# A delta-rule recurrence's triangular system: three products on the right-hand side in place of the block inverse

## The chip, the cores and the metric

One Trainium2 chip, one core. The metric is the device time of one launch in microseconds. The kernel before took 2555.1 us (median of three runs, 2553.93 to 2557.61). Times in the text are microseconds; positions such as "1572 us" count from the start of the profiled execution's span.

## The reference, cut to what matters

The program is two blocks on a sequence of 256 tokens and 2048 channels in float32. The first block has two gated-linear-attention and pooling layers; the second has a mixer of an RWKV-7 group (16 heads of 64) beside a sparse-attention group, then cross attention and an MLP. The change touches the RWKV-7 recurrence alone:

```python
def step(state, inp):
    r_t, w_t, k_t, v_t, kk_t, a_t = inp
    sa = jnp.einsum('bhvk,bhk->bhv', state, -kk_t)
    state = (state * w_t[:, :, None, :]
             + sa[..., None] * (kk_t * a_t)[:, :, None, :]
             + v_t[..., None] * k_t[:, :, None, :])
    return state, jnp.einsum('bhvk,bhk->bhv', state, r_t)
```

The state is read by every step before it is updated, so a chunk of tokens computed at once leads to a triangular system: with N the strictly lower-triangular matrix of the scores between the removal keys within the chunk (128x128 for each head), one needs G = (I - N)^-1 applied to a right-hand side.

## The kernel before, in words

The whole program is one launch. Python code emits instructions, and a planner at build time fixes the order of each engine's queue from the program order, estimated costs and free buffers; semaphores between the engines are generated. Big projections (`project`) stream weights from HBM in 512 KB pieces, split them on ScalarE (L148) and VectorE (L154) into two parts and multiply three times (L163 to L165). The planner fills these products into holes of other stages.

`rwkv_half(hf, ...)` (L1269) handles 8 of the 16 heads, and is called twice: for the first half at L1546, for the second at L1665. Its steps are: decay and key preparation on all engines; the score products `psa` for all heads and both chunks of 128 tokens (L1402, kept in `sas`); the inverse of every 32x32 diagonal block of I - N, for all heads at once, by 30 steps on VectorE (L1407 to L1418), with the result in `invt` and, transposed, in `invx`; then, for two head groups of four heads each (`heads4`, L1422), the rest of the solve and the output. The two groups run as coroutines that take turns at each `yield` (`together`, L1510), so their instructions alternate in program order. Each goes through the chunks t = 0 and t = 1 in order, as the state s0 of the first enters the second. At t = 0 the right-hand side has 64 columns per head (the values), at t = 1 it has 128 (the values and the keys that meet the state).

For one head group and one chunk, the solve before the change is this. `spread` (L1431) puts the 32x32 block inverses on the diagonal of a 128x128 matrix per head: `wt` from `invt`, `xt` from `invx`. Then two levels, l = 5 (blocks of 64) and l = 6 (blocks of 128): `pz` = N times xt (L1451), masked to the level's off-diagonal blocks into `zt` (L1453), `pw` = zt times wt (L1457), added to `wt` (L1458). Between the levels `wt` is transposed on TensorE (`px`, L1445) and copied by ScalarE to `xt` (L1447). Then `pk` (L1462) makes the right-hand side `rhs` (L1464, and L1467 on GpSimd for t = 1), and `pg` = wt times rhs (L1471) is copied to `ga` (L1473). What follows, the masked scores `psr`/`sr`, `py`, `pst` and `s0`, isn't touched. All these tiles of 128x512 have tag "m", of which there are nine buffers; all PSUM results have tag "side", of which there are three. An fp32 product is two passes of TensorE, and each shows as an instruction.

After both groups are through, VectorE normalises y and the rope work of the attention projections follows; the latter shares a tag of two buffers ("rp") with the states s0.

Of the kernel before, what the change touches and what calls it, by code (L numbers as in the profile page):

```python
# [12 lines left out]
AL = mybir.AluOpType  # L13
# [11 lines left out]
C_IDENT, C_LT, C_GT, C_ONES, C_BD32, C_LE, C_SEL2, C_SEL4, C_FREQ, C_SEL8, C_ID32, C_ALL = (  # L25
    0, 128, 256, 384, 512, 640, 768, 770, 772, 796, 828, 860)
# [28 lines left out]
def tile_kernel(ctx: ExitStack, tc: tile.TileContext, I: dict, out: bass.AP):  # L55
    nc = tc.nc
    V, S, G, PE = nc.vector, nc.scalar, nc.gpsimd, nc.tensor
# [25 lines left out]
    def tl(tag, shape=None, dt=F, name=None):  # L83
        pool, (n, bufs) = (sb, BASE[tag]) if tag in BASE else (phase[1], phase[2][tag])
        shape = [128, n] if shape is None else shape
        return pool.tile(shape, dt, name=name or tag, tag=tag, bufs=bufs)

    def pconst(shape, name, dt=F):
        return phase[1].tile(shape, dt, name=name, bufs=1)

    def psum(tag, shape=None, name=None):
        return phase[3].tile(shape or [128, 512], F, name=name or tag, tag=tag, bufs=phase[4][tag])
# [4 lines left out]
    def pside(shape=None, name="side"):  # L97
        return psum("side", shape, name)
# [4 lines left out]
    def const(shape, name, dt=F):  # L103
        return sb.tile(shape, dt, name=name, bufs=1)
# [3 lines left out]
    cst = const([128, C_ALL], "cst")  # L108
    nc.sync.dma_start(cst[:, :128], I["cst"][:, :128])
    ident = cst[:, C_IDENT:C_IDENT + 128]  # L110
# [361 lines left out]
    for g in range(4):  # L472
        m = tl("g", [128, 2, 512], name="mem")
# [50 lines left out]
    for j, (t0, nt) in enumerate(PARTS):  # L524
# [15 lines left out]
        for cb in range(4):  # L540
            acc = [pacc() for _ in range(4)]
            for k0 in range(t0, t0 + nt, 2):
                wh, wl = load_w(we, k0, 2, cb * 512, 512)
                for t in range(4):
                    x = uT if t < 2 else ucT
# [20 lines left out]
    lev = const([128, 7 * 128], "lev", U8)  # L566
# [39 lines left out]
    for d in range(2):  # L606
        for half in range(2):
            w = gate_w(d, half)
            la = []
            for t in range(2):  # L610
                px = pside()
                PE.matmul(px, rT[:, 1, t * 128:(t + 1) * 128], w, start=True, stop=True)
                x = tl("h", name="lac")
# [281 lines left out]
    for p in range(2):  # L895
# [12 lines left out]
        for q in (0, 2):  # L908
            pt = transpose2(lambda t, kt: of[:, t, kt * 128:(kt + 1) * 128], q)
            h, l = ybT.h[p][:, q:q + 2], ybT.l[p][:, q:q + 2]  # L910
# [93 lines left out]
    class Rows:  # L1004


        n = 4
# [194 lines left out]
    seg2 = tl("c", name="seg2")  # L1202
    G.memset(seg2, 1.0)
    G.memset(seg2.rearrange("p (n c) -> p n c", c=128)[:, :, 0:1], 0.0)
    strict = cst[:, C_LT:C_LT + 128]
    upto = cst[:, C_LE:C_LE + 128]
    bc4 = lambda m: m[:, None, :].to_broadcast([128, 4, 128])
# [61 lines left out]
    def rwkv_half(hf, kx, rx, vx):  # L1269
# [6 lines left out]
        for dst, p0, b0 in ((sgm, 0, W0), (av, 64, A0)):  # L1276
            for q in (0, 2):
                pd = pside([128, 2, T], name="pd")
                for r in range(2):
                    PE.matmul(pd[:, r], wup[p0:p0 + 64, (q + r) * 128:(q + r + 1) * 128], lora[p0:p0 + 64, 0],  # L1280
                              start=True, stop=True)
# [101 lines left out]
        def scores(dst, qx_, mask, hg, t, name):  # L1383

            ps = [pside([128, 2, 2, 128], name="p" + name) for _ in range(2)]
            for n, kx_ in enumerate((av, kx)):
                for c in range(2):
                    for o in range(2):
                        PE.matmul(ps[o][:, n, c], head(kx_, hg, 2 * c + o, t), head(qx_, hg, 2 * c + o, t), start=True, stop=True)
            for o in range(2):  # L1390
                V.tensor_tensor(dst(o).rearrange("p a b i -> p (a b) i"), ps[o].rearrange("p a b i -> p (a b) i"), bc4(mask),
                                op=AL.mult)
# [15 lines left out]
        for j in range(1, 31):  # L1408
            n = 31 - j
# [5 lines left out]
        invt = tl("g", [128, 32, 32], name="invt")  # L1415
        invx = tl("g", [128, 32, 32], name="invx")
# [5 lines left out]
        def heads4(hg):  # L1422
            s0 = None
            for t in range(2):
                tok = slice(t * 128, (t + 1) * 128)
                hv = slice(hg * 256, hg * 256 + 256)
                sa = sas[t, hg]
                nt_ = lambda i: sa[:, i % 2, 0, i // 2]
                b0 = (t * 2 + hg) * 4

                def spread(x, name):  # L1431
                    d = tl("m", [128, 4, 128], name=name)
                    V.tensor_tensor(wide(d), x[:, :, b0:b0 + 4].rearrange("p i h -> p h i")[:, :, None, :].to_broadcast([128, 4, 4, 32]),
                                    wide(bc4(cst[:, C_BD32:C_BD32 + 128])), op=AL.mult)
                    return d


                wt = spread(invt, "wt")
                xt = spread(invx, "xt")
                for l in range(5, 7):  # L1440
                    yield
                    if l == 6:
                        px = pside([128, 4, 128], name="px")
                        for i in range(4):
                            PE.transpose(px[:, i], wt[:, i], ident)  # L1445
                        xt = tl("m", [128, 4, 128], name="xt")
                        S.copy(xt, px)  # L1447
                        yield
                    pz = pside([128, 4, 128], name="pz")
                    for i in range(4):  # L1450
                        PE.matmul(pz[:, i], nt_(i), xt[:, i], start=True, stop=True)  # L1451
                    zt = tl("m", [128, 4, 128], name="zt")
                    V.tensor_tensor(zt, pz, bc4(lev[:, l * 128:(l + 1) * 128]), op=AL.mult)  # L1453
                    yield
                    pw = pside([128, 4, 128], name="pw")
                    for i in range(4):
                        PE.matmul(pw[:, i], zt[:, i], wt[:, i], start=True, stop=True)  # L1457
                    V.tensor_tensor(wt, pw, wt, op=AL.add)  # L1458
                yield
                pk = pside([128, 4, 64], name="pk")  # L1460
                for i in range(4):
                    PE.matmul(pk[:, i], sa[:, i % 2, 1, i // 2], vn[:, t, hg * 256 + i * 64:hg * 256 + i * 64 + 64], start=True, stop=True)  # L1462
                rhs = tl("m", [128, 4, 128], name="rhs")
                V.tensor_copy(rhs[:, :, :64], pk)  # L1464
                n = 128 if t else 64
                if t:
                    G.tensor_copy(rhs[:, :, 64:], an[:, hv].rearrange("p (h k) -> p h k", h=4))  # L1467
                yield
                pg = pside([128, 4, 128], name="pg")
                for i in range(4):  # L1470
                    PE.matmul(pg[:, i, :n], wt[:, i], rhs[:, i, :n], start=True, stop=True)  # L1471
                ga = tl("m", [128, 4, 128], name="ga")
                S.copy(ga[:, :, :n], pg[:, :, :n])  # L1473
                yield
                sr = [tl("m", [128, 2, 2, 128], name="sr") for _ in range(2)]
                scores(lambda o: sr[o], rx, upto, hg, t, "sr")
                if t:
                    yield
                    pr_ = pside([128, 2, 128], name="pr_")
                    for i in range(4):  # L1480
                        c, o = divmod(i, 2)
                        PE.matmul(pr_[o * 64:o * 64 + 64, c], ga[:, i, 64:], sr[i % 2][:, 0, i // 2], start=True, stop=True)
                    rh = tl("m", [128, 2, 128], name="rh")
                    V.tensor_tensor(rh, pr_, rx[:, hg * 2:hg * 2 + 2, tok], op=AL.add)
                yield
                py = pside([128, 4, 64], name="py")
                for i in range(4):
                    c, o = divmod(i, 2)
                    PE.matmul(py[:, i], sr[o][:, 0, c], ga[:, i, :64], start=True, stop=False)
                    PE.matmul(py[:, i], sr[o][:, 1, c], vn[:, t, hg * 256 + i * 64:hg * 256 + i * 64 + 64], start=False,  # L1490
                              stop=t == 0)
                    if t:
                        PE.matmul(py[:, i], rh[:, c], s0[:, c, o], start=False, stop=True)
                S.copy(y[:, t, hv], flat(py))
                if t == 0:
                    yield
                    pst = pside([128, 2, 64], name="pst")
                    for i in range(4):
                        c, o = divmod(i, 2)
                        hk = slice(hg * 256 + i * 64, hg * 256 + i * 64 + 64)  # L1500
                        PE.matmul(pst[o * 64:o * 64 + 64, c], bn[:, hk], ga[:, i, :64], start=True, stop=False)
                        PE.matmul(pst[o * 64:o * 64 + 64, c], kn[:, hk], vn[:, 0, hk], start=False, stop=True)
                    s0 = tl("rp", [128, 2, 2, 64], name="s0")
                    G.memset(s0, 0.0)
                    for c in range(2):
                        for o in range(2):
                            r = slice(o * 64, o * 64 + 64)
                            S.activation(s0[r, c, o], pst[r, c], AF.Identity, scale=fs[r, hg * 2 + c:hg * 2 + c + 1])

        for _ in together(*[heads4(hg) for hg in range(2)]):  # L1510
            pass
# [221 lines left out]
    for hf in range(2):  # L1733
        for q in (0, 2):
            pt = transpose2(lambda t, kt: yr[hf][:, t, kt * 128:(kt + 1) * 128], q)
            h, l = yrT.h[hf][:, q:q + 2], yrT.l[hf][:, q:q + 2]
# [176 lines left out]
```

## Time and profile before

| | us |
|---|---|
| median of three runs | 2555.1 |
| profiled execution | 2557.92 |
| its span | 2556.2 |
| TensorE matmuls busy | 2422.8 (95%) |
| TensorE weight loads busy | 1928.6 (75%) |
| VectorE busy | 1796.2 (70%) |
| ScalarE busy | 1170.2 (46%) |
| GpSimd busy | 172.1 (7%) |

The page's chain of work that ended last is TensorE for 61% of the span, VectorE for 18% and waits for transfers for 11%. Matmul ends are modelled, so busy TensorE time overlaps itself; the start-to-start times in the chain are the better measure. The two calls of `heads4` run at 1361 to 1412 us and at 1572 to 1619 us.

### The profile page before, as it was taken

What the parts mean: (1) busy time and instruction counts of PE and PEld (TensorE: products, weight loads), DVE (VectorE), ACT (ScalarE), POOL (GpSimd) and SP (SyncE); (2) the same over time, 40 slices, a digit from 0 to 9 for tenths busy, and PEclk for the clock granted to TensorE, in tenths of its full rate; (3) what the DMA queues carried; (4) which work ended last, traced back from release to release, by engine and by line L of the source; (5) the groups of instructions that cost most, each with busy time, mean ns of one, the idle gap of its engine ahead of it and who ended that gap; (6) DMA issues with size and microseconds to landing.
All of it is one profiled execution on the core that took longest, in us unless ns stands there. A gap on an engine that the chain in (4) does not pass through costs nothing.

```text
span 2556.2 us, 32427 instructions
## 1 busy us (share of the span) xinstructions
PE 2422.8 (95%) x11491; PEld 1928.6 (75%) x11491; DVE 1796.2 (70%) x2991; ACT 1170.2 (46%) x1560; POOL 172.1 (7%) x169
## 2 busy tenths in 40 slices
PE   8999998889989998998999999999999999999998
PEld 5667766778767776787878677787888888888886
DVE  5898657997897888967687978755655544555544
ACT  6543244444653544445642452445544433444433
POOL 0000010220230010002020120100000000000000
PEclk9999999999999999999999999999999999999999
DMA  7877547676656788755633243145466555666554
GB/s 262 276 251 225 170 153 242 218 232 228 198 183 218 233 282 288 259 182 158 198 94 110 80 136 99 63 163 192 133 189 182 186 187 187 189 184 187 201 188 154
DMA packets 267358, 483.11 MB, mean 189 GB/s; under 512 B 21137, under 2 KB 45547, under 8 KB 267195
## 3 DMA queue, kind: packets, MB, share of 16 engines
q1 hardware_dynamic: 266875, 480.60, 58.4%
q8 instruction: 90, 1.47, 0.2%
q14 instruction: 73, 0.60, 0.1%
q10 hardware_dynamic: 320, 0.44, 0.1%
HBM read 477.82 MB, written 3.15 MB: 188 GB/s over the span
## 4 chain that ended last, share of the span: by engine, by line
PE 61%; DVE 18%; DMA 11%; issue 6%; ACT 3%; POOL 1%; SPq 0%; DVEq 0%; ACTq 0%; POOLq 0%
PE acc L165 17%; PE acc L164 17%; PE acc L163 17%; DMA ar<-in_w_ada 8%; DVE wl L154 6%; DVE aa L405 3%; PE trp L236 2%; ACT wh L148 1%; DMA lnb<-in_ln_b 1%; PE pw L1457 1%; PE pz L1451 1%; DVE u L1411 1%; DVE inv L1412 1%; DMA wr<-in_w_in_e 1%; DMA wr<-in_w_in_o 0%
## 5 line engine op out<-in xcount | busy, mean ns | idle before, releaser
L148 ACT CAST wh<-wr 128x1024 fp32r<-128x1024 f32 (+2 forms) x736 | 760.3, 1038 | 991.6 <-PE acc L165 804.6
L164 PE MATMUL acc<-wl,xh 128*128 128x512 f32 (+2 forms) x2560 | 1005.5, 393 | 22.9 <-DVE wl L154 22.7
L163 PE MATMUL acc<-wh,xh 128*128 128x512 f32 (+2 forms) x2560 | 1011.8, 396 | 14.1 <-ACT xh L253 6.1
L165 PE MATMUL acc<-wh,xl 128*128 128x512 f32 (+2 forms) x2560 | 1003.5, 393 | 2.4 <-DVE xl L254 1.9
L154 DVE TENSOR_TENSOR wl<-wr,wh 128x512 fp32r<-128x512 f32 (+2 forms) x928 | 622.3, 702 | 176.8 <-ACT wh L148 176.1
L164 PEld LDWEIGHTS acc<-wl,xh 128*128 128x128 f32 x2560 | 485.1, 189 | 135.8 <-DVE wl L154 37.2
L151 DVE TENSOR_TENSOR wl<-wr,wh 128x1024 fp32r<-128x1024 f32 x272 | 333.3, 1225 | 357.4 <-ACT wh L148 355.4
L163 PEld LDWEIGHTS acc<-wh,xh 128*128 128x128 f32 x2560 | 484.6, 189 | 127.1 <-ACT wh L148 10.0
L165 PEld LDWEIGHTS acc<-wh,xl 128*128 128x128 f32 x2560 | 484.8, 189 | 106.3 <-issue 4.0
L405 DVE SCALAR_TENSOR_TENSOR aa<-ar,cs,aa 128x512 f32<-128x512 f32 x240 | 191.0, 796 | 72.8 <-DMA ar<-in_w_ada 71.5
L165 PE MATMUL acc<-wh,ucl 128*128 128x512 f32 x128 | 50.9, 398 | 0.0
L164 PE MATMUL acc<-wl,uch 128*128 128x512 f32 x128 | 50.7, 396 | 0.0
L163 PE MATMUL acc<-wh,uch 128*128 128x512 f32 x128 | 49.8, 389 | 0.0
L381 DVE SCALAR_TENSOR_TENSOR am<-ar,cs,am 128x512 f32<-128x512 f32 x60 | 42.6, 746 | 7.3 <-DMA ar<-in_w_ada 7.3
L722 PE MATMUL pp<-eq,ek 128*128 128x128 f32 x224 | 29.4, 286 | 6.1 <-DVE ek L734 6.1
L722 PEld LDWEIGHTS pp<-eq,ek 128*128 128x128 f32 x224 | 28.5, 201 | 8.4 <-issue 5.0
L1055 POOL TENSOR_TENSOR sgo<-sgo,psc 128x512 f32<-128x512 f32 x8 | 14.6, 1850 | 295.5 <-ACT sgo L1049 164.8
L350 PE MATMUL ada<-wl,c 128*4 128x512 f32 x64 | 26.0, 406 | 4.2 <-DVE wl L154 4.2
L164 PE MATMUL acc<-wl,dh 128*128 128x512 f32 x64 | 26.2, 410 | 3.8 <-DVE wl L154 3.7
L457 DVE SCALAR_TENSOR_TENSOR xl<-trp,pr,xh 128x256 fp32r<-128x256 f32 x48 | 22.3, 480 | 10.1 <-ACT xh L456 9.9
L1866 ACT ACTIVATE un<-acc,rml 128x512 f32<-128x512 f32 x32 | 22.0, 689 | 15.6 <-PE acc L165 15.6
L163 PEld LDWEIGHTS acc<-wh,uch 128*128 128x128 f32 x128 | 24.4, 191 | 5.6
(592 smaller groups left out, 2457.3 us busy)
## 6 DMA issues: line engine op xcount, KB each, us to landing
ar<-in_w_ada SPq DMA_DIRECT2D x288, 256.0 KB
wr<-in_w_in_e SPq DMA_DIRECT2D x128, 512.0 KB
wr<-in_w_up SPq DMA_DIRECT2D x128, 512.0 KB
wr<-in_w_down SPq DMA_DIRECT2D x128, 512.0 KB
wr<-in_w_in SPq DMA_DIRECT2D x80, 512.0 KB
wr<-in_w_in_o SPq DMA_DIRECT2D x64, 512.0 KB
wr<-in_w_ada SPq DMA_DIRECT2D x64, 256.0 KB
wr<-in_w_out_e SPq DMA_DIRECT2D x32, 512.0 KB
```

What stands on the lines that cost most here:

```text
L148: S.copy(wh, wr)
L151: engines[0].tensor_tensor(wl, wr, wh.bitcast(F), op=AL.subtract)
L154: engines[q % 2].tensor_tensor(wl[:, q], wr[:, q], wh[:, q].bitcast(F), op=AL.subtract)
L163: PE.matmul(acc, xh, wh, start=start, stop=False)
L164: PE.matmul(acc, xh, wl, start=False, stop=False)
L165: PE.matmul(acc, xl, wh, start=False, stop=stop)
L236: PE.transpose(pt[:, q, t * 128:(t + 1) * 128], src(t, kt + q), ident)
L350: PE.matmul(acc, c4[:, k0 + q], wl[:, q], start=False, stop=k0 + q == 15)
L381: V.scalar_tensor_tensor(acc[a], w[:, q], col, acc[a], op0=AL.mult, op1=AL.add)
L405: V.scalar_tensor_tensor(acc, w, cs[:, k:k + 1], acc, op0=AL.mult, op1=AL.add)
L722: PE.matmul(pp[:, h, t], kx[:, 2 * h + c, s * 128:(s + 1) * 128], qx[:, 2 * h + c, t * 128:(t + 1) * 128], start=c == 0, stop=c == 1)
L1411: V.tensor_tensor(u, inv[:, j + 1:, j:j + 1].to_broadcast([128, n, j]), inv[:, j:j + 1, :j].to_broadcast([128, n, j]), op=AL.mult)
```

## The change

Off the diagonal blocks no inverse is formed any more. Let D be the block-diagonal matrix of the 32x32 inverses and M = D times the part of N outside the diagonal blocks. Then (I - N)^-1 b equals D applied to a solution that is built from b by repeated multiplication; as four block rows make the fourth power of the block-strict part vanish, three products are enough. `dt` and `dx` are the spread blocks (as wt and xt before). `pmm` multiplies dx with N, and a mask `off32` (one minus the mask of the 32x32 diagonal blocks, a new constant, made once at the start of the phase) keeps the blocks off the diagonal: `mt`. `pk` and `rhs` follow as before. Then x = rhs, and three times x = rhs + M x: `px` on TensorE, the add on VectorE, with a `yield` before each. Last `pg` = dt times x. The transposes, the ScalarE copy, the level masks and the second pair pz/pw are gone.

```diff
+    off32 = pconst([128, 128], "off32")
+    V.tensor_scalar(off32, cst[:, C_BD32:C_BD32 + 128], -1.0, 1.0, op0=AL.mult, op1=AL.add)
...
-                wt = spread(invt, "wt")
-                xt = spread(invx, "xt")
-                for l in range(5, 7):
-                    yield
-                    if l == 6:
-                        px = pside([128, 4, 128], name="px")
-                        for i in range(4):
-                            PE.transpose(px[:, i], wt[:, i], ident)
-                        xt = tl("m", [128, 4, 128], name="xt")
-                        S.copy(xt, px)
-                        yield
-                    pz = pside([128, 4, 128], name="pz")
-                    for i in range(4):
-                        PE.matmul(pz[:, i], nt_(i), xt[:, i], start=True, stop=True)
-                    zt = tl("m", [128, 4, 128], name="zt")
-                    V.tensor_tensor(zt, pz, bc4(lev[:, l * 128:(l + 1) * 128]), op=AL.mult)
-                    yield
-                    pw = pside([128, 4, 128], name="pw")
-                    for i in range(4):
-                        PE.matmul(pw[:, i], zt[:, i], wt[:, i], start=True, stop=True)
-                    V.tensor_tensor(wt, pw, wt, op=AL.add)
+                dt = spread(invt, "dt")
+                dx = spread(invx, "dx")
+                pm = pside([128, 4, 128], name="pmm")
+                for i in range(4):
+                    PE.matmul(pm[:, i], dx[:, i], nt_(i), start=True, stop=True)
+                mt = tl("m", [128, 4, 128], name="mt")
+                V.tensor_tensor(mt, pm, bc4(off32), op=AL.mult)
                 yield
                 pk = pside([128, 4, 64], name="pk")
...
+                x = rhs
+                for _ in range(3):
+                    yield
+                    px = pside([128, 4, 128], name="px")
+                    for i in range(4):
+                        PE.matmul(px[:, i, :n], mt[:, i], x[:, i, :n], start=True, stop=True)
+                    x = tl("m", [128, 4, 128], name="x")
+                    V.tensor_tensor(x[:, :, :n], px[:, :, :n], rhs[:, :, :n], op=AL.add)
                 yield
                 pg = pside([128, 4, 128], name="pg")
                 for i in range(4):
-                    PE.matmul(pg[:, i, :n], wt[:, i], rhs[:, i, :n], start=True, stop=True)
+                    PE.matmul(pg[:, i, :n], dt[:, i], x[:, i, :n], start=True, stop=True)
```

## Rows read from the trace of the kernel before

**Rows 1.** Busy time by stretch: PE, PEld, DVE, ACT, POOL, granted clock, DMA share, GB/s.
```profile
1411.00:1440.00 29.00, 26.11 (x127) 17.54 (x126) 27.86 (x100) 11.77 (x23) 7.06 (x6) 0.94 0.24 66
1440.00:1500.00 60.00, 57.37 (x263) 44.74 (x263) 45.97 (x119) 33.72 (x49) 1.91 (x4) 1.00 0.48 146
1572.00:1592.00 20.00, 17.59 (x137) 16.79 (x138) 11.64 (x18) 1.92 (x4) 0.00 (x0) 0.84 0.00 1
...
1601.00:1619.00 18.00, 17.30 (x159) 15.93 (x157) 8.82 (x17) 3.23 (x6) 1.04 (x1) 1.00 0.06 19
1619.00:1635.00 16.00, 11.20 (x51) 6.60 (x50) 15.73 (x58) 4.86 (x7) 6.18 (x5) 1.00 0.00 2
1660.00:1720.00 60.00, 60.00 (x293) 49.92 (x293) 35.54 (x67) 31.30 (x53) 0.00 (x0) 1.00 0.47 160
```

**Rows 2.** Chain of waits, second half, t = 0: start us, us, what.
```profile
1573.99 3.91 PE pz L1451 x16
1577.90 2.13 PE pw L1457 x16
1580.06 0.70 DVE wt L1458
1580.81 0.66 PE px L1445 x4
1581.46 1.89 PE pz L1451 x16
1583.35 1.94 PE pw L1457 x16
1585.30 1.73 PE pk L1462 x16
1587.03 1.79 PE pg L1471 x16
```

**Rows 3.** Chain of waits, second half, t = 1.
```profile
1599.01 2.20 PE pw L1457 x16
...
1606.46 1.73 PE pk L1462 x16
1608.20 1.84 PE pg L1471 x16
```

**Rows 4.** Chain of waits, first half: level-5 pw, a projection product, pk; then t = 1.
```profile
1367.66 1.78 PE pw L1457 x16
...
1369.68 0.23 PE acc L164
...
1375.80 1.73 PE pk L1462 x16
...
1390.21 1.16 PE pw L1457 x8
...
1398.24 1.73 PE pk L1462 x16
```

**Rows 5.** Timeline, second half, t = 0, one hand-over: start us, us, instruction, idle before.
```profile
1581.30 2.05 PE L1451 MATMUL pz<-xt,sa 128*128 128x128 f32 x16
...
1582.44 0.69 DVE L1453 TENSOR_TENSOR zt<-pz,lev 128x512 f32<-128x512 f32 x1 [1.69 <-PE pz L1451]
1583.19 2.11 PE L1457 MATMUL pw<-wt,zt 128*128 128x128 f32 x16
```

**Rows 6.** Projection products on TensorE in two stretches of the first half: us, busy, count.
```profile
1367.66:1375.80 8.14, 1.88 (x6) 1.00 0.62 184
1390.21:1398.24 8.03, 1.66 (x5) 1.00 0.01 2
```

**Rows 7.** Groups by line and shape, 1572 to 1619: busy us, mean ns, idle before.
```profile
L1451 PE MATMUL pz<-xt,sa 128*128 128x128 f32 x64 | 10.2, 322 | 4.9 <-DVE xt L1433 4.9
L1453 DVE TENSOR_TENSOR zt<-pz,lev 128x512 f32<-128x512 f32 x8 | 5.5, 691 | 5.8 <-PE pz L1451 5.8
...
L1484 DVE TENSOR_TENSOR rh<-pr__13355,rr 128x256 f32<-128x256 f32 x1 | 0.4, 415 | 0.0
```

## The prediction

> **What bounds the kernel now.** I read the page's table of slices first: TensorE is at nine tenths or more almost throughout, so the end belongs to whatever keeps TensorE from its next product, and the question is whether the triangular solve is such a place. So next the busy time by stretch [rows 1]. In the second half the solve runs from 1572 to 1619 us; TensorE is busy 17.59 of 20.00 us and 17.30 of 18.00 us there, VectorE about half the time, ScalarE and the DMA engines hardly at all. Then the chain of waits, read inside the solve in order of time [rows 2 to 4]: it is a sequence of TensorE groups pz, pw, px, pz, pw, pk, pg, each "x16" (two head groups of four heads, two passes for each fp32 product) and each starting where the one before ends. The two head groups alternate: while TensorE works for one, VectorE masks or adds for the other. A hand-over taken from the timeline shows that this just fits [rows 5]: a pair of groups takes 1.89 us, so one group 0.95; pz of group A starts at 1581.30, its mask runs from 1582.44 for 0.69, and pw of A starts at 1583.19, when pz of B has been issued. The solve is therefore bound by the number of TensorE passes, with one hole at the transposes (below). Behind it stand 16 us in which VectorE is the bound (15.73 of 16.00) and which begin when the solve is over, then TensorE without a gap (60.00 of 60.00) [rows 1]; after the first half, VectorE 27.86 of 29.00 and TensorE 57.37 of 60.00. The DMA engines are busy for less than half of these stretches [rows 1], so no transfer should take over as the bound, and what the solve gives up should reach the end.
>
> **What is removed.** For each half of the heads and each token chunk t (four solves): pw of level 5, the add into wt, the transposes px with the ScalarE copy xt, pz of level 6 with its mask, pw of level 6 with its add. In the second half, t = 0, this is the stretch from 1577.90 (pw) to 1585.30 (pk) [rows 2]: 7.40 us, namely 2.13 + 0.70 + 0.66 + 1.89 + 1.94 and the hand-overs. The 0.70 and 0.66 are the hole: eight transposes are too little work to cover the other group's add and copy. For t = 1 it is 1599.01 to 1606.46, 7.45 us [rows 3]. In the first half the same stretch is 1367.66 to 1375.80, 8.14 us, and 1390.21 to 1398.24, 8.03 us [rows 4], but TensorE put six and five products of the projection into it [rows 6], and these must be done in any case. They start 0.23 us apart where the chain shows them alone [rows 4], so 1.4 and 1.15 us come off: 6.75 and 6.9 us.
>
> **What is added.** The old first pz becomes pmm and its mask zt becomes mt: the same eight products, the same 128x512 mask (0.691) [rows 7]; I count no difference. New are three rounds of eight products M x with an add of rhs. For t = 0 the moving side has 64 columns; the nearest rows are pk and pg of the same shape, 1.73 and 1.79 us [rows 2], so 1.76 each, 5.3 for three. For t = 1 it has 128; pg of that shape takes 1.84 [rows 3] and pw 1.94 [rows 2]; I take 1.9, 5.7 for three. pg itself and pk are unchanged. Each round adds a wait: the products of one group wait for VectorE's add of that group, and behind them on TensorE's queue stand the other group's products, then the score products. With 64 columns the add is like rh (128x256 from PSUM, 0.415) [rows 7] and is covered by 0.87 us of the other group; with 128 columns it is the 0.69 us of zt, covered as at that hand-over [rows 5], without a margin to speak of.
>
> **Sum.** Second half: 5.3 - 7.4 = -2.1 and 5.7 - 7.45 = -1.75. First half: 5.3 - 6.75 = -1.45 and 5.7 - 6.9 = -1.2. Together -6.5 us on a path that TensorE sets.
>
> **What counts nothing.** ScalarE loses eight copies of some 0.6 us, but it sits idle in the solve [rows 1]; their effect is in the hole already. VectorE's work per solve goes from eight operations of 0.69 to two of 0.69 and six of 0.42 at t = 0, and stays at eight of 0.69 at t = 1; it has room in the second half, and in the first the weight splits use it. The one new constant off32 is a 128x128 operation, done once, with no neighbour waiting; bound 0 to 0.4 (twice its size, rh, takes 0.415 [rows 7]). The nine buffers of tag m: dt, mt, rhs and x of both groups are eight live tiles, and x of one round takes the place of the last but one, which TensorE has read by then, so I see no wait for a buffer, though with one spare only. pk needs nothing of the inverse any more and stands third instead of sixth among the solve's PSUM tiles. At t = 0 its first half could run in TensorE's idle 4.9 us ahead of the first product [rows 7]: bound 0 to -0.87 us per half, -1.7 in all. I take 0, as its rhs copy would then enter a stretch full of VectorE work.
>
> **Bounds of the disputed price,** a round. Below: pk's 1.73 for both widths, which makes twelve rounds 20.8 us instead of 22.0 (sum -7.7). Above: the add isn't covered at all, and each round shows 0.9 us of VectorE (0.69 and some 0.2 of hand-over, from its times [rows 5]): +10.8 us, sum +4.3. I take the rows' alternation, because pz and pw with the same mask or add run without a hole in it.
>
> [...] A 64-column pass of pk takes 1.73 / 16 = 0.108 us and a 128-column pass of pw 1.94 / 16 = 0.121 [rows 2]: twice the columns, 12% more time. [...]
>
> **Rivals.**
> 1. The rounds wait for the adds: the groups fall out of step (a buffer of tag m released late, or the planner's order putting both adds behind one another), and each of the twelve rounds shows 0.9 us. For it: the hand-over fits [rows 5] within 0.1 us, and one spare buffer; against it: the same handshake holds today. It would give +4.3 us, 2559; it turns the change slower once the waits exceed 0.55 us a round, which is 6.5 / 12.
> 2. The gain is eaten on the way: the planner orders the neighbouring projection and rope work anew, or the first half's part (-2.65) is lost where the projection's products filled holes. -1 to -4.5, about 2552. For it: the first half's TensorE had other work to fill with [rows 6]. Against it: both halves are followed by VectorE at its limit [rows 1].
> 3. pk moves ahead at t = 0 in both halves: -6.5 - 1.7 = -8.2, 2547.
> 4. Time goes with the columns moved: 64-column rounds at half of pw's 1.94, 0.97 instead of 1.76, for six rounds: a further -4.7, -11.2 in all, 2544. pk and pg with 64 columns speak against it.
>
> **How the numbers follow.** The profiled execution took 2557.9 us (span 2556.2), 2.8 above the median of the three runs, 2555.1; the forecast is a difference, so 2555.1 - 6.5 = 2548.6, say 2549. What can't be told from no change is 0.2%, 5.1 us: faster means below 2550.0, slower above 2560.2. Chances: the forecast 0.52 (its own range 2546 to 2551.5), rival 1 0.16, rival 2 0.24, rival 3 0.05, rival 4 0.03. Faster: 0.44 of the forecast's 0.52 and rivals 3 and 4, 0.52. Slower: half of rival 1, in which a round shows more than one add, 0.08, and 0.04 of rival 2, a new order that costs more than all the solves give; 0.12. Same: the rest, 0.36. The range for 8 in 10 goes from rival 4 to just below rival 1: 2543 to 2558.
>
> **What would show it.** In the solve the chain should read pmm, pk, three rounds px, pg, the rounds 1.7 to 1.95 us each for both groups and with no VectorE entry between them. From pg's end to the first product of its solve it should be shorter by 2 us in the second half and by 1.3 in the first, and VectorE's full stretches should follow as much earlier. VectorE's adds between the px entries of the chain, or px's waits above 0.5 us, would show rival 1; solves shorter by 6 us with the same end, rival 2. The forecast is wrong if a round takes over 2.2 us or if the end moves less than the solves.

## The result, and the profile after

The changed kernel took 2570.93 us (median of eight executions, 2568.13 to 2583.57), the kernel before 2556.36 beside it; the ratio is 1.0054, with a 95% interval of 1.0038 to 1.0070. That is 14 us slower by the interval's middle, where 6.5 us faster was forecast. The profiled execution took 2576.02 us, its span 2574.3 (2556.2 before).

In the page's 40 slices of the kernel after, two digits show at once where to look: slices 25 and 26, from 1545 to 1673 us, are the only ones in which the clock granted to TensorE is under nine tenths. They hold the solve of the second half.

```profile
PEclk9999999999999999999999997899999999999999
```

The busy time by stretch of the kernel after (columns as in [rows 1]) answers to the rows 1572 to 1592 and 1601 to 1619 there, in which the clock was 0.84 and 1.00.

```profile
1572.00:1592.00 20.00, 14.33 (x66) 14.09 (x66) 8.21 (x13) 0.00 (x0) 0.00 (x0) 0.50 0.01 4
...
1600.00:1612.00 12.00, 12.00 (x73) 11.54 (x72) 5.32 (x9) 0.93 (x3) 0.60 (x2) 0.50 0.01 1
1612.00:1616.00 4.00, 2.83 (x24) 2.42 (x23) 2.98 (x4) 2.09 (x8) 0.20 (x1) 0.59 0.00 0
1616.00:1627.00 11.00, 10.55 (x90) 10.16 (x90) 6.00 (x10) 0.79 (x2) 0.00 (x0) 1.00 0.00 0
```

From 1570.9 to 1615.2 us the clock granted to TensorE was 0.50, and from 1580 to 1612 TensorE had no gap. Before the change the clock was 0.50 from 1571.65 to 1578.47: it came up 4.5 us after the first product, which starts at 1573.99. In steps of 0.5 us from 1564 to 1588 (before) and of 1 us from 1566 to 1624 (after) it reads 0.50 or 1.00, and something between only in the steps in which it changes (0.65 and 0.53 before, 0.93 and 0.88 after). So the mean of a longer stretch is read below, as an estimate, as a share of these two; in the kernel before, 0.69 over 4 us is 2.5 us at 0.50:

```profile
1572.00:1576.00 4.00, 2.01 (x9) 1.96 (x10) 3.71 (x5) 0.00 (x0) 0.00 (x0) 0.50 0.00 0
1576.00:1580.00 4.00, 4.00 (x26) 3.92 (x26) 2.08 (x3) 0.00 (x0) 0.00 (x0) 0.69 0.02 4
```

The chain of waits of the kernel after, second half, t = 0 and then t = 1, answers to [rows 2, 3]:

```profile
1574.95 2.06 PE pmm L1444 x8
...
1579.72 2.05 PE pmm L1444 x8
1581.77 3.31 PE pk L1450 x16
1585.08 10.24 PE px L1461 x48
1595.32 3.41 PE pg L1467 x16
1598.73 4.86 PE psr L1391 x31
...
1611.72 2.02 PE pmm L1444 x8
...
1617.58 1.73 PE pk L1450 x16
1619.32 5.78 PE px L1461 x48
1625.10 1.94 PE pg L1467 x16
```

The order of work is the one forecast (pmm, pk, three rounds px, pg, no VectorE entry between the rounds), but at t = 0 pk takes 3.31 us where [rows 2] have 1.73, and the three rounds 10.24 where 5.3 was forecast. At t = 1, with the clock back, they take 5.78 (forecast 5.7). (In the new code M is the part of N outside the diagonal blocks times D, in this order, and D is applied once more at the end.)

How it began shows in VectorE's timeline of the kernel before (start us, us, instruction, idle before), where the spreads of both head groups come ahead of the first mask:

```profile
1571.95 0.97 DVE L1433 TENSOR_TENSOR wt<-invt,cst 128x512 f32<-128x512 f32 x1
1572.84 1.01 DVE L1433 TENSOR_TENSOR xt<-invx,cst 128x512 f32<-128x512 f32 x1
1573.76 1.02 DVE L1433 TENSOR_TENSOR wt<-invt,cst 128x512 f32<-128x512 f32 x1
1574.69 1.02 DVE L1433 TENSOR_TENSOR xt<-invx,cst 128x512 f32<-128x512 f32 x1
1576.08 0.69 DVE L1453 TENSOR_TENSOR zt<-pz,lev 128x512 f32<-128x512 f32 x1 [0.37 <-PE pz L1451]
```

In the timeline of the kernel after, VectorE and TensorE at the same place:

```profile
1573.80 1.00 DVE L1435 TENSOR_TENSOR dx<-invx,cst 128x512 f32<-128x512 f32 x1
...
1574.95 2.05 PE L1444 MATMUL pmm<-sa,dx 128*128 128x128 f32 x8 [4.89 <-DVE dx L1435]
1577.04 0.69 DVE L1446 TENSOR_TENSOR mt<-pmm,off 128x512 f32<-128x512 f32 x1 [2.23 <-PE pmm L1444]
1577.64 1.01 DVE L1435 TENSOR_TENSOR dt<-invt,cst 128x512 f32<-128x512 f32 x1
1578.57 1.01 DVE L1435 TENSOR_TENSOR dx<-invx,cst 128x512 f32<-128x512 f32 x1
...
1579.72 2.05 PE L1444 MATMUL pmm<-sa,dx 128*128 128x128 f32 x8 [2.72 <-DVE dx L1435]
```

The old code handed over to the other group between the spreads and the first product (the `yield` at the head of the level loop); the new code has none there. So the mask mt of group A stands on VectorE's queue ahead of dt and dx of group B. VectorE idles 2.23 us for A's product, TensorE 2.72 us for B's spread, and the full-width products come in two bursts of eight instead of one of sixteen.

The second half, from its first product to the end of its last pg, took 36.1 us before and 52.1 after. By starts from the two chains and the timelines, in us:

| second half | before | after | difference |
|---|---|---|---|
| first products up to what follows them, t = 0 | 3.91 | 6.82 | +2.9 |
| the same, t = 1 | 2.3 | 5.9 | +3.6 |
| removed stretches, both chunks | 14.85 | | -14.85 |
| three rounds, t = 0 and t = 1 | | 10.24 + 5.78 | +16.0 |
| pk and pg, t = 0 | 3.52 | 6.72 | +3.2 |
| score, output and state products between pg and t = 1 | 7.9 | 12.9 | +5.1 |
| pg, t = 1 | 1.84 | 1.94 | +0.1 |
| sum | | | +16.0 |

The spans differ by 18.1; the rest lies outside this solve, 2.1 us of it ahead of the first half's transposes (invt starts at 1358.2 before and 1360.3 after).

In the first half the stretch between the starts of the two calls' transposes invt took 209.6 us against 210.8: nothing was lost there in this execution. The split is there too (pmm at 1365.37 and at 1370.72), but the planner had put twelve projection products between the two bursts; TensorE did not stand idle between them, and the clock, at 0.50 from 1366.1, was up at 1369.5.

### The profile page after: what moved, and what is told of

Same layout as the page of the kernel before. It is cut to its first block, busy times and chain, and to the rows that moved or that the text cites. A ratio compares the mean times of both kernels' runs of the same rounds, so it can differ in the third digit from the quotient of the medians.

```text
span 2574.3 us, 32337 instructions
## 1 busy us (share of the span) xinstructions
PE 2444.3 (95%) x11459; PEld 1950.4 (76%) x11459; DVE 1790.7 (70%) x2992; ACT 1164.4 (45%) x1550; POOL 174.5 (7%) x169
## 4 chain that ended last, share of the span: by engine, by line
PE 66%; DVE 18%; DMA 9%; issue 4%; ACT 2%; POOL 1%; SPq 0%; DVEq 0%; ACTq 0%; POOLq 0%
PE acc L163 18%; PE acc L165 18%; PE acc L164 18%; DMA ar<-in_w_ada 7%; DVE wl L154 5%; DVE aa L405 3%; PE trp L236 2%; PE px L1461 1%; ACT wh L148 1%; DMA wr<-in_w_in_o 1%; DMA lnb<-in_ln_b 1%; DVE u L1413 1%; DVE inv L1414 1%; PE ada L350 0%; PE psr L1391 0%
```

## Experiments

Two theories. **The order**: the split pair of pmm costs its own idle time, and is why the clock is not raised. **The columns**: the solve now begins at 0.50 and goes on with passes of 64 columns, during which the clock stayed there; before the change pz, pw and pz again had 128. The stage times below run from the first pz or pmm to the end of the last pg in the profiled execution; "before" is the kernel before on the same chip.

| kernel | median us | before | ratio (95%) | first half | second half |
|---|---|---|---|---|---|
| before (first profile) | | | | 39.0 | 36.1 |
| changed | 2570.9 | 2556.4 | 1.0054 (1.0038 to 1.0070) | 40.3 | 52.1 |
| e1_yield | 2566.3 | 2558.8 | 1.0020 (1.0004 to 1.0036) | 35.6 | 33.5 |
| e1_again | 2585.2 (one) | 2562.5 | | 51.3 | 47.2 |
| e2_cols | 2562.3 | 2558.8 | 1.0017 (1.0004 to 1.0031) | 40.2 | 41.0 |
| e3_gap | 2565.7 | 2558.8 | 1.0025 (1.0012 to 1.0037) | 42.2 | 43.8 |
| e4_both | 2558.5 | 2558.8 | 0.9995 (0.9979 to 1.0012) | 35.5 | 33.8 |
| w4_warm2_yield | 2556.6 | 2562.5 | 0.9978 (0.9960 to 0.9996) | 35.6 | 33.1 |
| w5_warm2_after | 2562.0 | 2562.5 | 0.9998 (0.9984 to 1.0012) | 40.2 | 39.2 |
| w6_warm2_before | 2562.6 | 2562.5 | 0.9993 (0.9979 to 1.0008) | 39.1 | 35.8 |
| v1_cols_warm2 | 2553.8 | 2559.4 | 0.9976 (0.9959 to 0.9992) | 35.5 | 33.6 |
| v2_warm_both | 2559.4 | 2559.4 | 0.9999 (0.9983 to 1.0016) | 34.3 | 32.1 |
| v3_cols_warm_both | 2559.0 | 2559.4 | 0.9997 (0.9984 to 1.0011) | 34.3 | 33.6 |

The first half's invt starts anywhere between 1352.8 and 1366.3 us, ahead of all that the edits touch; so the times are read by their intervals and the stages by their own lengths. The ratio is not the quotient of the two medians beside it. The first half's stage also holds projection products that the planner put there, 0.23 us each from start to start (1572.77, 1573.00 and 1573.23 in v1, at a clock of 1.00): 19 in the kernel before and in w6, 34 in the changed kernel and in w5, 36 in e3, 29 in e2, 10 to 14 in the others. The second half's stage holds none, except for six in each of the kernels w4 to v3.

**e1_yield: the order mended.**
```diff
                 dx = spread(invx, "dx")
+                yield
                 pm = pside([128, 4, 128], name="pmm")
```


> The changed kernel with one yield more, between the spreads dt, dx and the product pmm, so that the spreads of both groups of heads stand on VectorE ahead of both masks mt, as they did before the change. Nothing else differs. Theory of the order (mt of the first group holds back the spreads of the second, TensorE runs 8 passes, stands idle, runs 8 passes, and the clock is not raised): the two pmm follow one another without a gap, TensorE's granted clock in the second half's solve rises to 1.0 within some 8 us of the first pmm as it did before the change, first product to rope falls from 59.9 us to about 41 to 43, and the time is 2549 to 2553 us. Theory of the columns (once the clock is at 0.50, passes of 64 columns do not bring it up): the clock stays at 0.50 until the 128-column products of the second chunk, first product to rope stays at 56 to 60 us, and the time is 2565 to 2571 us.

The profiled execution did what the theory of the order expects: 2550.3 us, with the chain of waits

```profile
1569.69 3.94 PE pmm L1445 x16
1573.63 2.54 PE pk L1451 x16
1576.17 5.36 PE px L1462 x48
1581.53 1.79 PE pg L1468 x16
```

and the clock up during pk, 5.5 us after the start of the first pmm. But the other eleven took 2559.8 to 2572.4 us, with a mean granted clock of 0.972 to 0.978 over the span where the profiled one had 0.982 and 35 executions of the kernel before had 0.978 to 0.984. With the order mended the kernel still loses in most executions; neither theory's number holds for all of them.

**e1_again: the same kernel, another execution.**

> A second look at the changed kernel with the yield between the spreads and pmm: the same kernel, another execution. Its eleven other timed executions lay at 2560 to 2572 us with a mean clock of 0.972 to 0.978. If 64-column passes do not bring the clock up, such an execution has it still at 0.50 when pk begins, and then through pk, px and pg of the first chunk, some 35 us from the start of pmm; TensorE has no gap in it. If it is something else (another stretch of the kernel, DMA), the second half's solve looks as in the first look, 33.5 us from the first pmm to the last pg, and the clock is lost elsewhere.

This execution (2585.2 us, clock 0.967) is what the theory of the columns expects, in both halves. Chain of waits, second half:

```profile
1590.14 3.92 PE pmm L1445 x16
1594.05 3.31 PE pk L1451 x16
1597.36 10.24 PE px L1462 x48
1607.60 3.41 PE pg L1468 x16
```

and busy time by stretch, first half and second:

```profile
1368.00:1390.00 22.00, 22.00 (x97) 21.11 (x98) 7.53 (x15) 1.63 (x3) 0.00 (x0) 0.50 0.23 69
...
1600.00:1612.00 12.00, 12.00 (x62) 11.88 (x63) 2.12 (x5) 0.74 (x2) 0.00 (x0) 0.50 0.00 0
1612.00:1624.00 12.00, 12.00 (x80) 11.66 (x79) 7.04 (x9) 0.74 (x2) 0.40 (x1) 0.50 0.00 1
1624.00:1628.00 4.00, 4.00 (x37) 3.88 (x35) 1.16 (x4) 2.47 (x8) 0.40 (x1) 0.68 0.00 0
```

pmm is one burst as in e1_yield and takes the same 3.9 us, VectorE's order is the same, TensorE has no gap, and the clock stays at 0.50 until the 128-column pmm of t = 1. The same happened in the first half, with a few 512-column projection products in between. So the order alone does not decide. This execution is slower than all twelve timed ones, so it does not stand for them as it is. As an estimate, 36 us at 0.50 in place of 1.00 take 0.007 off the mean clock of a span of 2560 us: the eleven, some 0.006 under the kernel before, fit one such stretch, where this execution has two.

The busy time that the profile shows did not go with the clock here: TensorE was busy 12.00 of 12.00 us, twice in a row, and the clock stayed at 0.50. As the ends of products are modelled (the first sixteen px show 3.62 us of busy time from 1597.15, and the next start 3.42 after them), the profile does not show how much of that time the array worked.

**e2_cols: full rounds, the order not mended.**
```diff
+                else:
+                    G.memset(rhs[:, :, 64:], 0.0)
...
-                        PE.matmul(px[:, i, :n], mt[:, i], x[:, i, :n], start=True, stop=True)
+                        PE.matmul(px[:, i], mt[:, i], x[:, i], start=True, stop=True)
...
-                    V.tensor_tensor(x[:, :, :n], px[:, :, :n], rhs[:, :, :n], op=AL.add)
+                    V.tensor_tensor(x, px, rhs, op=AL.add)
```


> The changed kernel with the three rounds of the first chunk on full tiles of 128 columns: the right-hand side's other 64 columns are set to zero on GpSimd, px and its additions run over all 128. The order on VectorE stays that of the changed kernel (mt of the first group ahead of the spreads of the second). Theory of the columns: the granted clock rises within some 8 us of the start of px in the second half, first product to rope falls by about 12 to 15 us to 45 to 48, and the time is 2556 to 2560 us. Theory of the order alone: the clock stays at 0.50 through the rounds, which then take longer than 10.2 us for 48 products, and the time is 2570 us or more.

Busy time by stretch, where px begins at 1590.62:

```profile
1588.00:1592.00 4.00, 4.00 (x20) 4.00 (x20) 0.89 (x3) 0.00 (x0) 0.00 (x0) 0.50 0.00 0
1592.00:1596.00 4.00, 4.00 (x32) 3.86 (x30) 2.32 (x4) 0.00 (x0) 0.00 (x0) 0.86 0.02 4
1596.00:1600.00 4.00, 4.00 (x38) 3.77 (x38) 1.83 (x3) 0.74 (x2) 0.00 (x0) 1.00 0.00 0
```

The clock stayed at 0.50 through both pmm and the 64-column pk and came up 2.5 us into the 128-column rounds (0.86 over 4 us is 1.1 us at 0.50), as the theory of the columns expects. The three rounds are still 48 passes, now of twice the width, and took 7.04 us instead of 10.24. The stage is 11 us shorter than in the changed kernel (52.1 to 41.0; 12 to 15 expected). The median, 2562.3, lies 2 us above the expected 2556 to 2560.

**e3_gap: the kernel before with the changed kernel's order.**
```diff
                 for l in range(5, 7):
-                    yield
+                    if l > 5:
+                        yield
```


> The kernel before, with the yield between the spreads wt, xt and the product pz left out at the first level, so that VectorE has zt of the first group ahead of the spreads of the second, as the changed kernel has mt. All products stay as before the change, with 128 columns. Theory of the order alone: the granted clock of the second half's solve stays at 0.50 for some 30 to 40 us, and the time is 2568 to 2574 us. Theory of the columns: the clock rises during pw, a few us later than before, and the time is 2557 to 2561 us.

```profile
1570.00:1576.00 6.00, 2.68 (x11) 2.45 (x12) 2.99 (x4) 0.00 (x0) 0.00 (x0) 0.50 0.00 0
1576.00:1580.00 4.00, 4.00 (x21) 4.00 (x21) 1.38 (x2) 0.00 (x0) 0.00 (x0) 0.50 0.02 4
1580.00:1584.00 4.00, 3.65 (x29) 3.39 (x29) 1.38 (x2) 1.17 (x2) 0.00 (x0) 0.94 0.00 0
...
1600.00:1604.00 4.00, 3.02 (x14) 3.05 (x15) 1.53 (x2) 0.11 (x1) 0.40 (x1) 0.62 0.00 0
```

By these stretches the clock is up by 1580.5, in pw (1577.4 to 1580.7), as the theory of the columns expects: with products of 128 columns after the gap it did not stay down. But the gap costs more than that theory's forecast allowed: 36.1 to 43.8 us for the stage. TensorE stands idle at t = 1 as well, for 2.2 us, and the clock fell once more there (0.62 in 1600 to 1604). 2565.7 lies between the two forecasts.

**e4_both: order and columns.** The edits of e1_yield and e2_cols together.

> The changed kernel with both edits: the yield between the spreads and pmm, and full 128-column rounds in the first chunk. By either theory the clock rises as before the change. The rounds of the first chunk then cost as those of the second (5.78 for 48 products in place of 5.2 at full clock). First product to rope 41 to 44 us, and 2549 to 2554 us.

The stage takes 33.8 us, and the median is that of the kernel before (0.9995; the interval goes from 5 us faster to 3 us slower), some 4 us above the upper end of what I expected. So both edits together take away the whole loss, but no gain is shown. Put beside one another, the four second halves sort the loss: 52.1 (changed), 41.0 (columns), 33.5 or 47.2 (order, in two executions), 33.8 (both). The split order costs 5 to 8 us in every pair (52.1 to 47.2, 41.0 to 33.8, 36.1 to 43.8); the clock at 0.50 through the 64-column products costs 11 to 14 (52.1 to 41.0, 47.2 to 33.5), in the profiled execution of the changed kernel and in one of two with the order mended. Each figure rests on one execution of a kernel; the medians, which all executions enter, go the same way (1.0054 changed, 1.0020 and 1.0017 with one edit, 0.9995 with both).

**The clock at the start of the solve.** These kernels add six products of 128x512 in the second half, whose result nothing uses, where TensorE otherwise stands idle for 4.9 us. With them the planner also moved eleven projection products that had run ahead of the transposes: five into that idle stretch and six into the solve behind it. w6, the kernel before with the same edit, has the same eleven and so stands against both.
```diff
+        for src, reps in ((flat(inv), 2), (flat(invt), 4)) if hf else ():
+            pwarm = pbg([128, 512], "pwarm")
+            for _ in range(reps):
+                PE.matmul(pwarm, src[:, :128], src[:, :512], start=True, stop=True)
```

w4_warm2_yield, with the order mended:

> The changed kernel with the yield between the spreads and pmm, and six extra products of 128x512 in float32, whose result nothing uses, in the second half alone, on inv and invt, where TensorE stands idle for 4.9 us before the first pmm. Nothing is left out. If the clock at the start of the solve decides, it is at 1.0 from pmm on in nearly every execution, first pmm to last pg is some 32 us (33.5 in the profiled run with the clock at 0.5 in its first 4.8 us), less up to 2 us by which the extra products may delay pmm; 2547 to 2553 us. If the extra products, themselves begun at a falling clock, last too long, pmm starts 4 us late or more and the time is 2555 us or more.

w5_warm2_after, on the changed kernel as it is:

> The changed kernel with the same six extra products in the second half, the order on VectorE not mended (mt of the first group ahead of the spreads of the second). If the clock at the start decides, it stays at 1.0 over the gap of some 3 us between the two pmm, first pmm to last pg is some 35 us, and the time 2550 to 2556 us. If the gap in itself costs the clock, it falls to 0.50 in it, the 64-column passes leave it there, first pmm to last pg is near 50 us and the time 2565 us or more.

w6_warm2_before, on the kernel before:

> The kernel before with the same six extra products in the second half. Its clock is at 0.50 for some 7 us from the first pz, in which pz takes 3.9 us and pw 2.1: with the clock up these would be some 2.0 and 1.9. At best 2 us off the time, 2556 to 2558 us beside a kernel before of 2558.8; if the extra products delay the first pz by 2 us or more, nothing or a loss of up to 3 us.

In w4 the clock is 1.00 in every stretch from 1572 to 1660 us, the stage takes 33.1 us, and the kernel is faster than the one before: 0.9978 (0.9960 to 0.9996), 2556.6 beside 2562.5. That is 4 us above the expected numbers, where the kernel before, too, took 4 us more. One of its twelve executions still took 2574.6 at a mean clock of 0.975; its first half has no extra products, but it was not profiled. w6 shows no gain from the extra products in the kernel before (0.9993, 0.9979 to 1.0008; the clock there was at 0.50 for 4.5 us from the first pz, not 7), and its median lies 6 us above that of w4 on the same chip, so w4's gain goes with the change and not with the extra products alone. In w5 the clock held at t = 0, and the 64-column rounds there ran at full rate (5.36 us). But the gap there was not the one of the changed kernel: the six projection products stood in it, and TensorE idled for 1.39 us instead of 2.72:

```profile
1568.95 1.13 PE L1448 MATMUL pmm<-sa,dx 128*128 128x128 f32 x8
1569.83 0.48 PE L163 MATMUL acc<-wh,xh 128*128 128x512 f32 x1
...
1572.86 1.13 PE L1448 MATMUL pmm<-sa,dx 128*128 128x128 f32 x8 [1.39 <-DVE dx L1439]
```

Its stretches at t = 1, where nothing stood in the gap, show where the clock was lost:

```profile
1592.00:1596.00 4.00, 1.76 (x13) 1.76 (x13) 2.62 (x4) 1.24 (x4) 0.00 (x0) 0.90 0.00 0
1596.00:1600.00 4.00, 4.00 (x21) 4.00 (x21) 1.04 (x3) 0.00 (x0) 0.00 (x0) 0.50 0.00 0
1600.00:1604.00 4.00, 4.00 (x27) 3.86 (x27) 2.08 (x3) 0.00 (x0) 0.00 (x0) 0.75 0.00 0
```

There TensorE idles 2.24 us for dx of group B; by these means the clock falls at 1595.2 and comes up at 1602.0, in the 128-column rounds. So what the gap alone does to a clock that begins at 1.00 shows at t = 1 only. The stage is 39.2 against 33.1 with the order mended; I had expected 35 and a faster kernel, and it is level with the one before.

**Versions that might beat both.** v1 has the yield, the full rounds and the six extra products; v2 the yield and extra products in both halves (three on invt in the first), with 64-column rounds; v3 all of it.

> The changed kernel with the yield, full 128-column rounds in the first chunk, and the six extra products ahead of the second half's solve. In the second half the clock is at 1.0 from the start, in the first half it can come up in the rounds where it had fallen. The rounds cost some 0.5 us more than with 64 columns. If the clock was all that the change lost, no execution has a solve with the clock at 0.50 for over 15 us, and the time is 4 to 7 us under the kernel before on the same chip; the spread of its executions is that of the kernel before. If full columns and extra products do nothing together that w4 did not, the median is that of w4, some 6 us under the kernel before, with single executions 15 us above it.

> The changed kernel with the yield and extra products ahead of both solves (six in the second half, three on invt in the first), 64-column rounds. In the second look at the kernel with the yield alone, the first half's solve too had the clock at 0.50 for some 35 us; here it starts at 1.0, unless the extra products delay the first pmm of the first half by more than the 2.4 us for which TensorE stands idle there. 5 to 8 us under the kernel before on the same chip, with no execution 10 us above the median. If the first half's fall of the clock is rare, the same median as w4.

> All three edits: the yield, full 128-column rounds in the first chunk, extra products ahead of both solves. By the theory of the columns with the clock at the start it has nothing left to lose but the 0.5 us per half for the wider rounds: within 2 us of v2 and with the narrowest spread of executions. If the wider rounds cost more than that, 2 to 4 us above v2.

v1 took 2553.8 us beside 2559.4: 0.9976 (0.9959 to 0.9992), some 6 us as expected. It can't be told from w4 (0.9978), so a gain of the full rounds on top of w4 is not shown; its slowest execution lies 8 us over its median, that of w4 18. The second half's solve runs at full clock:

```profile
1572.00:1592.00 20.00, 19.23 (x137) 15.81 (x135) 13.46 (x18) 0.74 (x2) 0.85 (x4) 1.00 0.09 27
1592.00:1612.00 20.00, 19.75 (x194) 18.60 (x193) 13.86 (x21) 4.38 (x12) 1.47 (x2) 1.00 0.01 2
```

v2 and v3 missed: their solves are as short or shorter, but the stretch between the end of the first half's pg and the second half's invt grew from 168.4 us in w4 and 169.2 in v1 to 178.3 and 177.1. In v2 the planner put thirteen projection products behind the first half's solve that in w4 run before its end, most of them ahead of the first pmm, and the clock was 0.86 from 1400 to 1440 us (0.96 in w4). As an estimate, thirteen products at 0.23 us are 3 us; and the means of the four stretches of 40 us from 1400 to 1560 (0.86, 0.93, 1.00, 0.96 in v2, 0.96, 0.96, 1.00, 0.96 in w4) come to some 20 us at 0.50 in v2 and some 10 in w4, and the 10 more cost up to 5. No run takes the two apart.

## Why the prediction was wrong

The step that failed is "The old first pz becomes pmm and its mask zt becomes mt: the same eight products, the same 128x512 mask (0.691) [rows 7]; I count no difference." The products and the mask are the same, but the hand-over ahead of them went, and with it VectorE's order. I had the 4.9 us of idle time before pz and the clock of 0.84 in [rows 1], and read neither the order of VectorE's queue from the new code nor in which products the clock came up in that stretch (in pw, at 1578.47). The pair of pmm cost 6.5 us more than I counted.

A second step failed with it: "so 1.76 each, 5.3 for three", a price from rows at full clock, set in without asking whether the new sequence reaches that clock. At t = 0 the three rounds took 10.24 us, and pk, pg and the products behind them 8.3 us more than before. Mending the order alone did not undo this (e1_again: 10.24 again).

**The rounds.** The price was right for a clock of 1.00, and this condition was not stated. At full clock three rounds of 64 columns took 5.36 us (e1_yield; 5.3 forecast) and three of 128 took 5.78 (5.7). At 0.50 they take 10.24. No round waited for an add: rival 1's mechanism did not appear, although the change did turn slower, as rival 1 had it. The groups by line of the kernel after, 1572 to 1632 us (busy us, mean ns, idle before), have no idle time before px, and the adds at the expected 0.42 and 0.69:

```profile
L1461 PE MATMUL px<-x,mt 128*128 128x64 f32 x32 | 7.0, 421 | 0.0
...
L1463 DVE TENSOR_TENSOR x<-px,rhs 128x512 f32<-128x512 f32 x6 | 4.1, 691 | 1.9 <-PE px L1461 1.9
L1461 PE MATMUL px<-x,mt 128*128 128x128 f32 x32 | 4.0, 281 | 0.0
...
L1463 DVE TENSOR_TENSOR x<-px,rhs 128x256 f32<-128x256 f32 x6 | 2.5, 424 | 7.7 <-PE px L1461 7.7
```

**The sum.** For the second half I forecast -3.85. Where the order is mended and the clock is up from pk on, the stage is 2.6 us shorter (33.5 against 36.1), and with the clock up throughout 2.7 (33.1 against 35.8 in w6): right in sign, two thirds in size. For the first half I forecast -2.65. The stage became shorter by up to 3.5 us (35.5 to 35.6 against 39.0), but it holds 12 to 14 projection products where it had held 19, which are 1.2 to 1.6 us, so some 2 us are the solve's own. From invt to invt the two halves lie 209.1 to 209.9 us apart in e1_yield, e4, w4 and v1 against 210.8 to 213.0 in the first profile, e3 and w6: 1 to 4 us. That projection products come after the solve instead of filling it is rival 2, in part. In all, the 6 us of w4 and v1 are near the 6.5 of the sum, but they need two and three edits that the change did not have, the extra products also moved projection products, and the intervals (1 to 10 us) are too wide to confirm the sum.

**What stays open.** In two executions of e1_yield's kernel the same sixteen products of 3.9 us were followed by a rise of the clock in one and not in the other; what decides between them no run shows. Nor does one show why e4, whose solves are as short as those of w4 and v1 within 1 us, is level with the kernel before. The other seven executions of the changed kernel were not profiled; their mean clock, 0.968 to 0.975, fits the profiled 0.971.

## What to carry to other kernels

When a change shortens a chain of TensorE work that starts after an idle time, read the granted clock at its start (here 0.50, after 4.9 us of idle time, before and after the change) and ask in which products it comes up now; a price taken from rows at full clock held here only where the new sequence got there (5.36 us against 10.24). When a loop head goes, the hand-over in it goes too: write down the order of each engine's queue around the first step that stays. Undoing one of the two faults alone left a loss, undoing both brought the change level with the kernel before, and only work in the idle stretch ahead of the solve, together with the mended order, brought about what its count of passes had promised (w4 and v1; in v2 and v3 it was lost in the stretch between the halves).

## What the hardware showed unexpectedly

- Products of 64 columns, or of 64 rows (psr), ran without a gap for 30 us at a granted clock of 0.50 (after, 1581.8 to 1611.7; e1_again, 1594.1 to 1624.8), and each pass took nearly twice its time at full clock (pk 3.31 against 1.73 us). Where the clock was at 1.00, it stayed there through the same products (e1_yield from 1575.2 on, w5 at t = 0).
- Where rounds of 128 columns began at 0.50, the clock came up in them (e2_cols after 2.5 us, w5 at t = 1 after 3.2).
- Gaps of 2.2 us on TensorE, with products of 64 columns ahead of them, were followed by a fall of the clock to 0.50 (e3_gap at 1601.0, w5 at 1595.2).
- 48 passes took 5.36 us with 64 columns (e1_yield, t = 0) and 5.78 with 128 (after, t = 1) at a clock of 1.00: half the columns save 7%.
